# A hybrid decoder layer on one core: operands placed on whole lines, low-part products last, S5 scans joined

## The chip, the core and the metric

The kernel runs on one core of one Trainium2 chip (trn2). The metric is device time in microseconds, the median of several executions. Engines are named as in the profile: PE is TensorE's matmul, PEld its weight load, DVE is VectorE, ACT ScalarE, POOL GpSimd, SP the engine that issues most DMAs.

## The reference

One layer on `x` of 256 tokens by 2048 channels, in float32: a SwiGLU feed-forward pass, a token mixer (four mLSTM heads beside 64 groups of S5 state-space channels), a second SwiGLU pass, each added to `x`, and a last norm.

```
x = x + 0.5 * swiglu(rms_norm(x, ffn1_norm), w1, w3, w2)        # 2048 -> 5632 -> 2048
h = rms_norm(x, mix_norm);  p = h @ w_in                        # q|k, v, o, i, f, u
hm = rms_norm(mlstm_chunkwise(silu(conv(qk)), v, i, f)) * sigmoid(o)
states = associative_scan(a * s + b u)                          # S5, complex diagonal, 64 states a group
hs = glu(gelu(real(C states) + d_skip * u))
x = x + concat([hm, hs]) @ w_out
x = x + 0.5 * swiglu(rms_norm(x, ffn2_norm), ...);  out = rms_norm(x, final_norm)
```

## The kernel before

All large products are made from two parts of each operand. A weight step (`fetch`, L148 to L157) loads 1024 columns' worth of weights per partition (two K tiles of 512, in the output-gate part two of 344) into `wraw`, ScalarE rounds them into the high part `whi` (L154, type fp32r), and VectorE subtracts to get the low part `wlo` (L156). TensorE then makes three products per operand pair: high by high, high by low, low by high. Three steps are fetched ahead (`AHEAD`, L141); `wraw` has four buffers, `whi` and `wlo` three each.

`step_tok` (L159) makes a step with the token side stationary: for each of two K tiles and two token tiles it issues (xh, whi), (xh, wlo), (xl, whi), a weight tile of 512 columns as the moving operand (L174). Stationary are `xh`/`xl` (the transposed, normed input) in w1, w3 and w_in, `gh`/`gl` (the feed-forward's hidden values) in w2, and `hmh`/`hml`, `hsh`/`hsl` (the mixer's two halves) in w_out. Only the first step of the kernel has its low-part products last (`lo_last`, L169). `gemm_ch` (L210) has the weight tile stationary and 256 tokens moving (L224 to L226), for u, q and k, and for the S5 gate with `yh`/`yl` moving. `tail` (L409) finishes the last 512 output columns with moving tiles of 256 columns (L474 to L476).

The mixer (L771) runs the w_in chunks in the order u, output gate with input and forget gates, q and k, v, then w_out. Between its steps other work is hung in: `after(n, ...)` runs a function n steps later (the gates, the convolutions, the heads), and `bg` hands out the S5 work, 0.62 pieces a step. For each of eight channel groups j, S5 is: `load` (DMAs of tables), `drive` (products with the input, four multiplications on VectorE at L849 to L852 into A0, A3, A1, A2, two additions on GpSimd, L853 and L854), `scan` (eight scans of 128 elements on VectorE, L860, from A0 to A1 and from A2 to A3), `unrotate` (six operations on GpSimd, L868 to L873, through tiles B0 and B1), `emit` and `act`. The convolution of one of eight q/k tiles is four operations on VectorE (L939, L942) and a Silu. The order of instructions is left to the framework's scheduler, but for SyncE's and the start's; each engine runs its own queue in order, so a subtraction for the weights stands behind whatever VectorE was given before it.

Tiles are placed in SBUF pool by pool, in the order in which the pools are opened, each tile rounded up to 32 bytes per partition: const, xp, xTp, wrawp, whip, wlop, small, junkp, s5p, and then the pools of a phase.

Of the kernel before, what the change touches and what calls it, by code (L numbers as in the profile page):

```python
# [37 lines left out]
AHEAD = 2  # L38
WARM = 7
# [20 lines left out]
class _Layer:  # L60
# [98 lines left out]
    def step_tok(self, acc, xs, part, w, n, first, last, lo_last=False):  # L159
# [26 lines left out]
    def start(self, acc, view, gain):  # L186

        W = lambda i: self.weights(view, i * KK, KK, 0, NC)
        M = lambda i, w: self.step_tok(acc, self.xs, [(i * KK, 0), (i * KK + 1, 0)], w, NC, i == 0, i == 7, i == 0)
# [20 lines left out]
    def gemm_ch(self, acc, xs, view, nk, c0):  # L210

        nc = self.nc
        for k0 in range(0, nk, KK):
            wh, wl = self.weights(view, k0, KK, c0, NC)
            for kk in range(KK):
                k = k0 + kk
                xh, xl = xs(k)
                sp = k == nk - 1
                for nt in range(4):
                    o = acc[nt // 2][:, (nt % 2) * S:(nt % 2 + 1) * S]  # L220
                    ns = slice(nt * P, (nt + 1) * P)
                    st = k == 0 and nt % 2 == 0
                    kw = dict(skip_group_check=True)
# [9 lines left out]
    def setup(self):  # L233
# [16 lines left out]
        vec0 = self.junkp.tile([KD, P], F32, name="vec0")  # L250
# [3 lines left out]
        idle = self.junkp.tile([P, NC], F32, name="junk")  # L254
# [8 lines left out]
        self.mhalf = c.tile([P, 8], F32, name="mhalf")  # L263
# [6 lines left out]
        vecs = self.junkp.tile([rows, P], F32, name="vecs")  # L270
# [500 lines left out]
    def mixer(self, chunk_done):  # L771
# [4 lines left out]
        with ExitStack() as ctx:  # L776
            mp = self.pool("mix", ctx=ctx)
# [18 lines left out]
            uT = [mp.tile([P, 4, 2, HC], F32, name=f"uT{i}", tag=f"uT{i}") for i in range(2)]  # L796
            u4 = [mp.tile([P, 8, HC], F32, name=f"u4{i}", tag=f"u4{i}") for i in range(2)]
# [14 lines left out]
            yT = mp.tile([P, NJ, S], F32, name="yT")  # L812
            yh = mp.tile([P, NJ, S], F32R, name="yh")
            yl = mp.tile([P, NJ, S], F32R, name="yl")
# [7 lines left out]
            def s5(j):  # L822
# [3 lines left out]
                def load():  # L826
# [9 lines left out]
                    Bt = [mp.tile([P, 4, HC], F32, name=f"B{i}") for i in range(2)]  # L836
                    env["t"] = rv, w1, w2, k0, At, Bt

                def drive():
                    rv, w1, w2, k0, At, Bt = env["t"]  # L840
# [15 lines left out]
                def scan():  # L856
                    rv, w1, w2, k0, At, Bt = env["t"]
                    for a in (0, 2):
                        for q in range(4):
                            V.tensor_tensor_scan(At[a + 1][:, q, :],  # L860
                                                 self.R[:, 4 * j + q:4 * j + q + 1].broadcast_to([P, HC]),
                                                 At[a][:, q, :], 0.0, op0=ALU.mult, op1=ALU.add)

                def unrotate():
                    rv, w1, w2, k0, At, Bt = env["t"]
                    cs, sn = rv[:, 0], rv[:, 1]
                    zr, zi = At[1], At[3]
# [7 lines left out]
                def emit():  # L875
                    rv, w1, w2, k0, At, Bt = env["t"]
# [51 lines left out]
            for i, part in enumerate(self.gates(mp, gt, Dm, em)):  # L928
                self.after(1 + 4 * i, part)
# [23 lines left out]
            for hf in range(2):  # L953
                acc = self.pair()
                self.gemm_ch(acc, self.xs, win, KD, QK0 + hf * NC)
                qkp[hf] = mp.tile([P, 4, S + 3], F32, name=f"qkp{hf}", tag=f"qkp{hf}")
# [4 lines left out]
                for i in range(4):  # L961
                    self.after(1 + i, lambda hf=hf, i=i: conv(hf, i))
# [37 lines left out]
            def heads_T(c):  # L1000
                hmh[c] = mp.tile([P, 4, S], F32R, name=f"hmh{c}", tag=f"qkp{c}")
                hml[c] = mp.tile([P, 4, S], F32R, name=f"hml{c}", tag=f"vx{c}")
# [15 lines left out]
            for c in range(2):  # L1018
                v = mp.tile([P, TT, 2, DV + 1], F32, name=f"vx{c}", tag=f"vx{c}")
# [37 lines left out]
            hsh = [mp.tile([P, 4, S], F32R, name=f"hsh{i}", tag=f"uT{i}") for i in range(2)]  # L1057
            hsl = [mp.tile([P, 4, S], F32R, name=f"hsl{i}", tag=f"u4{i}") for i in range(2)]
# [26 lines left out]
    def gates(self, mp, gt, Dm, em):  # L1085
# [3 lines left out]
        rows = mp.tile([H, 4, S], F32, name="g_rows", tag="vx1")  # L1089
        more = mp.tile([H, 4, S], F32, name="g_more", tag="qkp1")  # L1090
        E = mp.tile([H, NCK, S], F32, name="g_E", tag="vx0")
# [130 lines left out]
```

## Time and profile before

| | us |
|---|---|
| median of 3 runs | 1885.29 (1884.81 to 1885.33) |
| the profiled execution | 1883.44 |
| its span, first to last instruction | 1881.7 |
| TensorE busy | 1840.2 (98%) |
| VectorE busy | 1082.8 (58%) |
| ScalarE busy | 811.5 (43%) |
| GpSimd busy | 340.3 (18%) |

The feed-forward passes fill the span up to about 760 us and from about 1145 us on; the mixer lies between. Matmul records overlap each other, since matmuls are pipelined: how fast TensorE goes is read from the distance between two starts, not from the length of a record. A mean granted clock of 1.00 is 2.4 GHz, and 0.50 is 1.2 GHz.

### The profile page before, as it was taken

Reading aid. Unit: us, or ns where it says so; the run is one execution under the profiler, and the core shown is the slowest. Engines: PE = TensorE matmul, PEld = TensorE weight load, DVE = VectorE, ACT = ScalarE, POOL = GpSimd, SP = SyncE. Lnnn points to the kernel's source line nnn. Section 1 sums busy time; section 2 is a strip of 40 time slices with the busy share of each in tenths; the row PEclk is TensorE's granted clock in tenths of the full one; section 3 lists DMA queues with packets and bytes.
Section 4 is the critical chain, followed back from the end, with each engine's and each line's share of the span. In section 5 each row is a group of like instructions: output and inputs, shape, how many; then the busy total and the mean of one; then the engine's idle time right before and its main releaser. Section 6 shows DMA issues by size and latency. Waiting matters only on the chain.

```text
span 1881.7 us, 24161 instructions
## 1 busy us (share of the span) xinstructions
PE 1840.2 (98%) x9221; PEld 1539.7 (82%) x9221; DVE 1082.8 (58%) x1335; ACT 811.5 (43%) x970; POOL 340.3 (18%) x523
## 2 busy tenths in 40 slices
PE   9999999999999999988889999999999999999998
PEld 7888888888888888987778888888888888888887
DVE  5547865555555455577888765445444444444454
ACT  6444443334444444434544455444443334444343
POOL 3000999700000000166323200000000000000011
PEclk9999999999999999999999999999999999999999
DMA  8666666666666555776766556666665566666554
GB/s 261 190 189 188 200 208 216 236 197 201 189 194 197 186 194 189 206 156 179 158 155 178 168 178 204 190 190 190 190 190 185 187 188 190 190 190 190 190 188 148
DMA packets 191252, 358.27 MB, mean 190 GB/s; under 512 B 12320, under 2 KB 29344, under 8 KB 191008
## 3 DMA queue, kind: packets, MB, share of 16 engines
q1 hardware_dynamic: 186992, 344.58, 62.2%
q0 software_dynamic: 4000, 11.10, 1.8%
q8 instruction: 72, 1.18, 0.3%
q10 hardware_dynamic: 144, 1.05, 0.1%
q14 instruction: 44, 0.36, 0.1%
HBM read 344.62 MB, written 11.01 MB: 189 GB/s over the span
## 4 chain that ended last, share of the span: by engine, by line
PE 48%; DVE 5%; issue 1%; DMA 1%; ACT 1%; POOL 0%; ACTq 0%; POOLq 0%; DVEq 0%
PE accb L174 42%; DVE wlo L156 2%; DVE A L860 1%; PE accb L226 1%; PE accb L224 1%; PE accb L225 1%; DMA wraw<-in_w_in_dram 1%; DVE qkc L942 1%; PE tpb L486 1%; PE accb L474 0%; PE accb L476 0%; PE accb L475 0%; DVE qkc L939 0%; ACT whi L154 0%; PE tpb L845 0%
## 5 line engine op out<-in xcount | busy, mean ns | idle before, releaser
L156 DVE TENSOR_TENSOR wlo<-wraw,whi 128x1024 fp32r<-128x1024 f32 (+1 forms) x630 | 788.6, 1254 | 736.6 <-ACT whi L154 736.0
L154 ACT CAST whi<-wraw 128x1024 fp32r<-128x1024 f32 (+1 forms) x630 | 655.0, 1041 | 950.9 <-PE accb L174 856.9
L174 PE MATMUL accb<-wlo,xh 128*128 128x512 f32 (+1 forms) x1568 | 606.2, 387 | 17.1 <-DVE wlo L156 17.1
L174 PE MATMUL accb<-whi,xh 128*128 128x512 f32 (+1 forms) x1568 | 609.7, 389 | 0.0
L174 PE MATMUL accb<-whi,xl 128*128 128x512 f32 (+1 forms) x1568 | 605.6, 387 | 0.0
L174 PEld LDWEIGHTS accb<-wlo,xh 128*128 128x128 f32 x1568 | 296.0, 189 | 76.4 <-DVE wlo L156 20.1
L174 PEld LDWEIGHTS accb<-whi,xl 128*128 128x128 f32 x1568 | 296.2, 189 | 57.9
L174 PEld LDWEIGHTS accb<-whi,xh 128*128 128x128 f32 x1568 | 295.9, 189 | 58.0 <-ACT whi L154 1.1
L174 PE MATMUL accb<-whi,gh 128*128 128x512 f32 x664 | 263.7, 397 | 0.0
L174 PE MATMUL accb<-whi,gl 128*128 128x512 f32 x664 | 262.4, 395 | 0.0
L174 PE MATMUL accb<-wlo,gh 128*128 128x512 f32 x664 | 262.3, 395 | 0.0
L174 PEld LDWEIGHTS accb<-whi,gl 128*128 128x128 f32 x664 | 124.7, 188 | 30.2
L174 PEld LDWEIGHTS accb<-whi,gh 128*128 128x128 f32 x664 | 124.7, 188 | 29.7
L174 PEld LDWEIGHTS accb<-wlo,gh 128*128 128x128 f32 x664 | 124.7, 188 | 29.6
L1186 POOL TENSOR_TENSOR x<-x,fn 128x512 f32<-128x512 f32 x6 | 8.9, 1500 | 699.6 <-ACT junk L317 699.6
L696 POOL TENSOR_TENSOR tr<-s5rot,sp 128x128 f32<-128x128 f32 (+6 forms) x112 | 62.1, 555 | 151.9 <-DVE sp L636 148.4
L226 PE MATMUL accb<-xh,wlo 128*128 128x256 f32 x256 | 73.6, 288 | 6.6 <-DVE wlo L156 6.6
L224 PE MATMUL accb<-xh,whi 128*128 128x256 f32 x256 | 73.9, 289 | 0.0
L225 PE MATMUL accb<-xl,whi 128*128 128x256 f32 x256 | 73.0, 285 | 0.0
L757 POOL DMA_DIRECT2D spillw<-s5w x16 | 8.6, 541 | 274.6 <-ACT s5w L728 259.7
L697 POOL TENSOR_TENSOR tr<-s5rot,sp 128x128 f32<-128x128 f32 (+6 forms) x112 | 57.8, 517 | 0.0
L226 PEld LDWEIGHTS accb<-xh,wlo 128*128 128x128 f32 x256 | 49.6, 194 | 7.6 <-DVE wlo L156 7.6
(312 smaller groups left out, 1416.3 us busy)
## 6 DMA issues: line engine op xcount, KB each, us to landing
wraw<-in_ffn_w_dram SPq DMA_DIRECT2D x528, 512.0 KB, 3.7
wraw<-in_w_in_dram SPq DMA_DIRECT2D x48, 512.0 KB, 5.3
wraw<-in_w_out_dram SPq DMA_DIRECT2D x32, 512.0 KB, 3.7
wraw<-in_w_in_dram SPq DMA_DIRECT2D x24, 344.0 KB, 5.6
spillrot<-s5rot POOLq DMA_DIRECT2D x8, 512.0 KB, 5.3
spillw<-s5w POOLq DMA_DIRECT2D x16, 256.0 KB, 4.2
s5rot<-spillrot SPq DMA_DIRECT2D x8, 512.0 KB, 7.8
wraw<-in_w_glu_dram SPq DMA_DIRECT2D x8, 512.0 KB, 3.9
```

Of the source, the lines that this page charges most:

```text
L154: nc.scalar.copy(hi, raw)
L156: nc.vector.tensor_sub(lo, raw, hi.bitcast(F32))
L174: nc.tensor.matmul(acc[t][:, :n], lhsT=x, rhs=wt, start=first and t not in seen, stop=last and t not in left)
L224: nc.tensor.matmul(o, lhsT=wh[:, kk, ns], rhs=xh, start=st, stop=False, **kw)
L225: nc.tensor.matmul(o, lhsT=wh[:, kk, ns], rhs=xl, start=False, stop=False, **kw)
L226: nc.tensor.matmul(o, lhsT=wl[:, kk, ns], rhs=xh, start=False, stop=sp, **kw)
L486: nc.tensor.transpose(b[:, o:o + P], s[t][:, kt * P:(kt + 1) * P], self.ident)
L696: G.tensor_tensor(tr[0][:, :, :k], rv[:, 0, :, 0:k], u0, op=ALU.mult)
L697: G.tensor_tensor(tr[1][:, :, :k], rv[:, 1, :, 0:k], u1, op=ALU.mult)
L860: V.tensor_tensor_scan(At[a + 1][:, q, :], self.R[:, 4 * j + q:4 * j + q + 1].broadcast_to([P, HC]), At[a][:, q, :], 0.0, op0=ALU.mult, op ...
L942: V.scalar_tensor_tensor(o, src[:, w:w + S], self.col("conv_w", w * 8 + j), o, op0=ALU.mult, op1=ALU.add)
L1186: nc.gpsimd.tensor_tensor(self.x[c][:, t, :], self.x[c][:, t, :], self.fn[:, c * NC:(c + 1) * NC], op=ALU.mult)
```

## The change

Four edits.

*Order of products.* `step_tok` puts all products with `whi` first and those with `wlo` behind them in every step; `gemm_ch` does the same. `lo_last` is gone.

*Layout.* Pads and moves of tiles change where tiles start: `mhalf` takes 256 bytes more, `junk` 448 more, `vec0` and `vecs` move from the junk pool into the buffers of `s5k0`; the mixer's large tiles (`uT`, `u4`, `yT`, `yh`, `yl`, `qkp`, `vx` and the tiles that take their places) get a pool `ma` of their own, opened before `mix`, with `qkp` and `vx` padded to 1152 elements (`WIDE`); `dg` shares the buffers of `th`.

*S5 scans.* Four scans of 128 elements become one of 512, in place, with the factors in a tile `Rt` whose first column of each 128 is zero, so that the state starts anew there. ScalarE fills `Rt` once per j. B0 and B1 are no longer tiles of their own: `unrotate` writes its intermediate products into A1 and A3.

*Convolutions.* They are hung in at every second step (`1 + 2 * i`) instead of every step.

```diff
@@ step_tok
-        todo = []
+        todo, late = [], []
         for kk, (k, _) in enumerate(part):
             xh, xl = xs(k)
             for t in range(TT):
                 ts = slice(t * P, (t + 1) * P)
-                todo += [(t, xh[:, ts], wh[:, kk, :]), (t, xh[:, ts], wl[:, kk, :]), (t, xl[:, ts], wh[:, kk, :])]
-        if lo_last:
-            todo = todo[0::3] + todo[2::3] + todo[1::3]
+                todo += [(t, xh[:, ts], wh[:, kk, :]), (t, xl[:, ts], wh[:, kk, :])]
+                late += [(t, xh[:, ts], wl[:, kk, :])]
+        todo += late
@@ gemm_ch
                 for nt in range(4):
-                    nc.tensor.matmul(o, lhsT=wh[:, kk, ns], rhs=xh, start=st, stop=False, **kw)
-                    nc.tensor.matmul(o, lhsT=wh[:, kk, ns], rhs=xl, start=False, stop=False, **kw)
-                    nc.tensor.matmul(o, lhsT=wl[:, kk, ns], rhs=xh, start=False, stop=sp, **kw)
+                    st = k0 + kk == 0 and nt % 2 == 0
+                    nc.tensor.matmul(o(nt), lhsT=wh[:, kk, ns(nt)], rhs=xh, start=st, stop=False, **kw)
+                    nc.tensor.matmul(o(nt), lhsT=wh[:, kk, ns(nt)], rhs=xl, start=False, stop=False, **kw)
+            for kk in range(KK):
+                xh, xl = xs(k0 + kk)
+                sp = k0 + kk == nk - 1
+                for nt in range(4):
+                    nc.tensor.matmul(o(nt), lhsT=wl[:, kk, ns(nt)], rhs=xh, start=False, stop=sp, **kw)
@@ setup
-        vec0 = self.junkp.tile([KD, P], F32, name="vec0")
+        vec0 = self.s5p.tile([KD, P], F32, name="vec0", tag="s5k0")
-        idle = self.junkp.tile([P, NC], F32, name="junk")
+        idle = self.junkp.tile([P, NC + 112], F32, name="junk")[:, :NC]
-        self.mhalf = c.tile([P, 8], F32, name="mhalf")
+        self.mhalf = c.tile([P, 72], F32, name="mhalf")[:, :8]
-        vecs = self.junkp.tile([rows, P], F32, name="vecs")
+        vecs = self.s5p.tile([rows, P], F32, name="vecs", tag="s5k0")
@@ mixer
+            ma = self.pool("mixa", ctx=ctx)
             mp = self.pool("mix", ctx=ctx)
-                    dg = tp2.tile([P, P], F32, name="dg")
+                    dg = tp2.tile([P, S], F32, name="dg", tag="th")[:, :P]
-            uT = [mp.tile([P, 4, 2, HC], F32, name=f"uT{i}", tag=f"uT{i}") for i in range(2)]
+            uT = [ma.tile([P, 4, 2, HC], F32, name=f"uT{i}", tag=f"uT{i}") for i in range(2)]
...
+            Rt = [mp.tile([P, 4, HC], F32, name=f"Rt{i}") for i in range(2)]
+            for i in range(2):
+                G.memset(Rt[i][:, :, 0:1], 0.0)
@@ s5: load, scan, unrotate
-                    Bt = [mp.tile([P, 4, HC], F32, name=f"B{i}") for i in range(2)]
+                    A.copy(Rt[j % 2][:, :, 1:],
+                           self.R[:, 4 * j:4 * j + 4].unsqueeze(2).broadcast_to([P, 4, HC - 1]))
                     for a in (0, 2):
-                        for q in range(4):
-                            V.tensor_tensor_scan(At[a + 1][:, q, :],
-                                                 self.R[:, 4 * j + q:4 * j + q + 1].broadcast_to([P, HC]),
-                                                 At[a][:, q, :], 0.0, op0=ALU.mult, op1=ALU.add)
+                        x = At[a].rearrange("p q c -> p (q c)")
+                        V.tensor_tensor_scan(x, Rt[j % 2].rearrange("p q c -> p (q c)"), x, 0.0,
+                                             op0=ALU.mult, op1=ALU.add)
-                    zr, zi = At[1], At[3]
+                    zr, zi, Bt = At[0], At[2], (At[1], At[3])
@@ q and k
-                qkp[hf] = mp.tile([P, 4, S + 3], F32, name=f"qkp{hf}", tag=f"qkp{hf}")
+                qkp[hf] = ma.tile([P, WIDE], F32, name=f"qkp{hf}", tag=f"qkp{hf}")[:, :4 * (S + 3)].rearrange("p (j s) -> p j s", j=4)
-                    self.after(1 + i, lambda hf=hf, i=i: conv(hf, i))
+                    self.after(1 + 2 * i, lambda hf=hf, i=i: conv(hf, i))
```

## Rows read from the trace of the kernel before

**Rows 1.** The page: busy us (share of the span) xinstructions.

```profile
PE 1840.2 (98%) x9221; PEld 1539.7 (82%) x9221; DVE 1082.8 (58%) x1335; ACT 811.5 (43%) x970; POOL 340.3 (18%) x523
```

**Rows 2.** Waits on TensorE: who <- for whom: us in total, times, longest.

```profile
PE accb L174 <- DVE wlo L156: 18.4, 11, 5.1
PE accb L226 <- DVE wlo L156: 6.6, 5, 2.9
PE tpb L1105 <- DVE gt L924: 3.3, 1, 3.3
```

**Rows 3.** Stages: length, busy PE, PEld, DVE, ACT, POOL, clock, DMA share, GB/s.

```profile
780.00:1055.00 275.00, 245.05 (x1681) 220.04 (x1680) 220.65 (x324) 111.42 (x153) 124.55 (x93) 0.98 0.68 169
820.00:862.00 42.00, 31.58 (x235) 28.65 (x234) 29.70 (x37) 11.97 (x18) 23.12 (x18) 0.95 0.76 143
900.00:960.00 60.00, 53.68 (x400) 49.23 (x399) 53.22 (x96) 26.30 (x33) 18.50 (x15) 0.97 0.68 156
```

**Rows 4.** The same view of two stretches below full clock.

```profile
857.00:866.00 9.00, 6.78 (x27) 6.78 (x28) 7.88 (x9) 2.64 (x6) 7.77 (x6) 0.62 0.46 112
939.00:944.00 5.00, 5.00 (x32) 5.00 (x31) 5.00 (x8) 1.78 (x3) 0.00 (x0) 0.66 0.84 225
```

**Rows 5.** The chain that ended last, pieces: start us, us, what.

```profile
1145.00 43.54 PE accb L174 x192
...
1454.85 90.19 PE accb L174 x387
...
1106.02 11.24 PE accb L174 x48
...
1847.28 0.11 PE accb L474
...
1860.54 0.11 PE accb L474
```

**Rows 6.** Timeline of TensorE: start us, us, instruction; first and last of 24, of 21.

```profile
787.37 0.28 PE L224 MATMUL accb<-xh,whi 128*128 128x256 f32 x1
...
790.25 0.28 PE L224 MATMUL accb<-xh,whi 128*128 128x256 f32 x1
...
1062.81 0.39 PE L174 MATMUL accb<-whi,hml 128*128 128x512 f32 x1
...
1067.67 0.40 PE L174 MATMUL accb<-whi,hml 128*128 128x512 f32 x1
```

**Rows 7.** Groups of weight loads, whole span: xcount | busy us, mean ns | idle before.

```profile
L174 PEld LDWEIGHTS accb<-whi,xl 128*128 128x128 f32 x1568 | 296.2, 189 | 57.9
```

**Rows 8.** Timeline of ACT and DVE in an undisturbed w2 step: [idle before <-releaser].

```profile
1501.32 1.05 ACT L154 CAST whi<-wraw 128x1024 fp32r<-128x1024 f32 x1 [1.75 <-PE accb L174]
1502.40 1.23 DVE L156 TENSOR_TENSOR wlo<-wraw,whi 128x1024 fp32r<-128x1024 f32 x1 [1.57 <-ACT whi L154]
```

**Rows 9.** Timeline around the longest wait on TensorE.

```profile
853.68 4.73 DVE L860 TENSOR_TENSOR_SCAN A<-R,A 128x128 f32<-128x128 f32 x8 [0.81 <-POOL A L853]
...
859.23 0.65 PE L174 MATMUL accb<-wlo,xh 128*128 128x344 f32 x1 [5.11 <-DVE wlo L156]
```

**Rows 10.** Two lines with scans: ns min/median/max, first and last start.

```profile
L860 DVE TENSOR_TENSOR_SCAN A<-R,A x64: 391/394/1518, 803.0 to 1039.8; 128x128 f32<-128x128 f32 x64
...
L1115 DVE TENSOR_TENSOR_SCAN g_rows<-g_more,g_rows x1: 678/678/678, 895.9 to 895.9; 4x256 f32<-4x256 f32 x1
```

**Rows 11.** Groups of VectorE and ScalarE in the mixer, 790 to 1056 us.

```profile
L942 DVE SCALAR_TENSOR_TENSOR qkc<-qkp,cols,qkc 128x256 f32<-128x256 f32 x24 | 18.0, 775 | 0.0
L939 DVE TENSOR_SCALAR qkc<-qkp,cols 128x256 f32<-128x256 f32 x8 | 7.0, 891 | 0.0
...
L1025 ACT ACTIVATE vx<-accb,rstd 128x512 f32<-128x512 f32 x4 | 2.6, 684 | 1.0 <-PE accb L174 1.0
```

**Rows 12.** Timeline: the last GpSimd operation of a group, the next group's second multiplication.

```profile
815.13 1.79 POOL L873 TENSOR_TENSOR S<-B,B 128x512 f32<-128x512 f32 x1
...
818.96 0.68 DVE L850 TENSOR_TENSOR A<-tpb,s5rot 128x512 f32<-128x512 f32 x1
```

More of the change, by code (lines that the diff above doesn't have):

```diff
@@ L38 @@
 AHEAD = 2
+WIDE = 1152
 WARM = 7
@@ L157, in fetch, with step_tok @@
         return hi.rearrange("p (k n) -> p k n", n=n), lo.rearrange("p (k n) -> p k n", n=n)
-    def step_tok(self, acc, xs, part, w, n, first, last, lo_last=False):
+    def step_tok(self, acc, xs, part, w, n, first, last):
         nc = self.nc
         wh, wl = w
-        todo = []
+        todo, late = [], []
         for kk, (k, _) in enumerate(part):
@@ L793, in mixer @@
             self.after(7, make_rB)
-            uT = [mp.tile([P, 4, 2, HC], F32, name=f"uT{i}", tag=f"uT{i}") for i in range(2)]
-            u4 = [mp.tile([P, 8, HC], F32, name=f"u4{i}", tag=f"u4{i}") for i in range(2)]
+            uT = [ma.tile([P, 4, 2, HC], F32, name=f"uT{i}", tag=f"uT{i}") for i in range(2)]
+            u4 = [ma.tile([P, 8, HC], F32, name=f"u4{i}", tag=f"u4{i}") for i in range(2)]
             def evac_u(hf, acc):
@@ L810, in evac_u @@
                                             in_=uT[hf][q * 32:(q + 1) * 32, :, ta, :])
-            yT = mp.tile([P, NJ, S], F32, name="yT")
-            yh = mp.tile([P, NJ, S], F32R, name="yh")
-            yl = mp.tile([P, NJ, S], F32R, name="yl")
+            yT = ma.tile([P, NJ, S], F32, name="yT")
+            yh = ma.tile([P, NJ, S], F32R, name="yh")
+            yl = ma.tile([P, NJ, S], F32R, name="yl")
             Ss = [mp.tile([P, 4, HC + 1], F32, name=f"S{i}") for i in range(2)]
@@ L927, in mixer @@
             em = mp.tile([P, TT, H], F32, name="em")
-            for i, part in enumerate(self.gates(mp, gt, Dm, em)):
+            for i, part in enumerate(self.gates(ma, mp, gt, Dm, em)):
                 self.after(1 + 4 * i, part)
@@ L1000, in heads_T @@
             def heads_T(c):
-                hmh[c] = mp.tile([P, 4, S], F32R, name=f"hmh{c}", tag=f"qkp{c}")
-                hml[c] = mp.tile([P, 4, S], F32R, name=f"hml{c}", tag=f"vx{c}")
+                hmh[c] = ma.tile([P, 4, S], F32R, name=f"hmh{c}", tag=f"qkp{c}")
+                hml[c] = ma.tile([P, 4, S], F32R, name=f"hml{c}", tag=f"vx{c}")
                 for half in range(2):
@@ L1018, in mixer @@
             for c in range(2):
-                v = mp.tile([P, TT, 2, DV + 1], F32, name=f"vx{c}", tag=f"vx{c}")
+                v = ma.tile([P, WIDE], F32, name=f"vx{c}", tag=f"vx{c}")[:, :4 * (DV + 1)].rearrange("p (t h d) -> p t h d", t=TT, h=2)
                 G.memset(v[:, :, :, DV:], 1.0)
@@ L1054, in mixer @@
             self.drain_bg()
-            hsh = [mp.tile([P, 4, S], F32R, name=f"hsh{i}", tag=f"uT{i}") for i in range(2)]
-            hsl = [mp.tile([P, 4, S], F32R, name=f"hsl{i}", tag=f"u4{i}") for i in range(2)]
+            hsh = [ma.tile([P, 4, S], F32R, name=f"hsh{i}", tag=f"uT{i}") for i in range(2)]
+            hsl = [ma.tile([P, 4, S], F32R, name=f"hsl{i}", tag=f"u4{i}") for i in range(2)]
             def evac_glu(hf, acc):
@@ L1083, in mixer, with gates @@
                 chunk_done(c)
-    def gates(self, mp, gt, Dm, em):
+    def gates(self, ma, mp, gt, Dm, em):
         nc = self.nc
         V, G, A = nc.vector, nc.gpsimd, nc.scalar
-        rows = mp.tile([H, 4, S], F32, name="g_rows", tag="vx1")
-        more = mp.tile([H, 4, S], F32, name="g_more", tag="qkp1")
-        E = mp.tile([H, NCK, S], F32, name="g_E", tag="vx0")
+        rows = ma.tile([H, 4, S], F32, name="g_rows", tag="vx1")
+        more = ma.tile([H, 4, S], F32, name="g_more", tag="qkp1")
+        E = ma.tile([H, NCK, S], F32, name="g_E", tag="vx0")
         li, f, bc, M = (rows[:, i, :] for i in range(4))
```

23 lines of the change are left out of this document (10 added, 13 removed).

## The prediction

> **What bounds the kernel now.** First the busy shares [rows 1]: TensorE is busy in 1840.2 of 1881.7 us, so time can only come from its idle 41.5 us or from a shorter distance between two matmuls. Then the waits on TensorE [rows 2]: 25.0 us are waits for the low parts `wlo` that VectorE makes (L156), 3.3 us one wait for the gates. Then the stages [rows 3]: nearly all of this lies between 780 and 1055 us, in the mixer: of these 275 us TensorE is busy in 245.05, VectorE in 220.65. Then the granted clock [rows 4]: a stretch of 9 us shows a mean of 0.62, and two of 5 us (939 to 944, 973 to 978, the first is shown) 0.66, so part of each ran at 1.2 GHz, each around one of the longer waits. The lost share is 9 x 0.38 + 2 x 5 x 0.34 = 6.8 us, at most, since TensorE also idled in them.
>
> Last, the distance of matmuls, which the busy share does not show (records overlap: 387 ns long, less than 240 apart). In unbroken pieces of the chain, none of which ever leaves TensorE [rows 5], 192 products with `xh`, `xl` of 512 columns take 43.54 us, 226.8 ns each; 387 products with `gh`, `gl` take 90.19 us, 233.0 each; 48 with `hsh`, `hsl` 11.24 us, 234.2 each; 21 with `hmh`, `hml` 4.86 us, 231.4 each [rows 6]. Shape, type, clock and moving tiles are the same in all four. What differs is where the stationary tile lies. Adding up the tile sizes of the pools, `xh`, `xl`, `whi` and `wlo` start 256 bytes past a multiple of 512, `gh`/`gl` 320, `hsh`/`hsl` 352, `hm` tiles 0, 32 and 96. A 512-column product at one column a cycle of 2.4 GHz is 213.3 ns, so each has 13.5 to 21 ns on top, and the least where the start is a multiple of 256. With 256 columns (106.7 ns) it is 24 products in 2.88 us for the channel-major steps, 120.0 ns each [rows 6], and 39 triples in 13.26 us at the end of the kernel, 113.3 each [rows 5].
>
> **The change, part by part.**
>
> *Layout.* No instruction is added. By the pad sizes (`mhalf` 256 bytes, `junk` and its neighbours 576 less, `WIDE`, the pool `ma`) the weights, `xT`, `gh` and `gl` all start at multiples of 2048 bytes afterwards, the mixer's operands at multiples of 512. I take it that every stationary tile then behaves as the best placed one does now: `gh`/`gl` products go from 233.0 to 226.8 ns: 3 x 664 (by the loops) x 6.2 = 12.4 us; `hs` 3 x 64 x 7.4 = 1.4 us; `hm` 3 x 64 x 4.6 = 0.9 us. **14.7 us.** The `xh` products, 256 past before and 0 after, I leave at 226.8: no row shows an operand pair at 0, and `hml1`, the one tile at 0 now (among neighbours at 32), runs at the 231.4 of its group. Bounds: nothing gained, and a gain or loss of one step more on all products (rivals).
>
> *High parts first.* The same 12 (or 24) products a step in another order, each with a weight load of its own before and after [rows 7]; that the loads stay hidden I take from the 189 ns a load takes beside distances of 227 and more. What moves is when things are needed and freed. A step needs `wlo` at its 9th product instead of the 2nd, 7 x 227 ns = 1.6 us later (17th instead of 3rd of 24: 14 x 120 = 1.7 us; in the 344-column steps 1.1 us). `whi` comes free 4 products, 0.9 us, earlier, so the cast starts earlier: in the steady state the cast waits 1.75 us for TensorE and the subtraction 1.57 us for the cast [rows 8], so both have that much to spare. `wlo` comes free one product, 0.2 us, later; behind the subtraction that waits for it, VectorE holds the next S5 or convolution operation, and the 1.57 us cover it.
>  Where TensorE waits only because its operand stood behind a group of other VectorE work, this shift is a gain; where VectorE has more work than time, it is gained once. The stage from 820 to 862 us is of the first kind (VectorE 29.70 of 42), 900 to 960 of the second (53.22 of 60) [rows 3]. The longest wait shows the first kind: eight scans end at 858.41, then the subtraction, and the second product of the step starts at 859.23, 5.11 us late [rows 9]; needed 1.1 us later it is still about 4 us late. Of 25.0 us of `wlo` waits I take 10 away: 6 of the output-gate steps' 10.4, 3 of the 12 in the two q/k steps and the v step behind them, 1 of the rest. The ends: 3 us if nearly all is throughput, 22 if each wait gets its shift. Of the clock's 6.8 us I take 4; ends 0 and 6.8.
>
> *Scans end to end.* 64 scans of 128 become 16 of 512. The nearest rows [rows 10]: 391 to 394 ns for one of 128 alone, 678 for one of 256, so about (678 - 394)/128 = 2.2 ns an element, and for 512 an estimate of 678 + 256 x 2.2 = 1.25 us. In the trace eight take 4.73 us [rows 9], of which the first and the fifth lose about 1.1 us each beside GpSimd (1.5 for 0.39). Two of 1.25 us that lose the same are 4.7: **hardly less**. Ends: 2 us less of VectorE per channel group if one such loss goes, 1 us more if a longer scan meets a second GpSimd operation. I take 1 us on TensorE. Added: eight copies of R on ScalarE over 508 elements, nearest row 684 ns for 512 [rows 11], hidden in ScalarE's idle time (busy 111.42 of 275 us there [rows 3]); ahead of a cast one would delay it by less than the 1.75 us it has to spare. The two small GpSimd memsets are worth 0.2 us on an engine that idles there.
>
> *B tiles taken over by A1 and A3.* The next group's second VectorE multiplication now waits for the last GpSimd operation of the group before (L873) instead of the one ahead of it. In the closest case L873 ends at 816.92 and L850 starts at 818.96 [rows 12]: 2.0 us of cover. Without it up to the 1.79 us of L873 a group, with the weight subtractions queued behind on VectorE.
>
> *Convolutions every second step.* The same 32 VectorE operations; four groups spread over eight steps instead of four. Each is about 0.89 + 3 x 0.775 = 3.2 us beside GpSimd [rows 11]. The last one is now due one step before the scores that read it; VectorE runs a step or two ahead of TensorE, so I cost it at nothing; if it does not, TensorE waits up to 3 us once, with the next chunk's products behind it. The spread takes peaks off, which is part of the 3 us above. The gates' wait of 3.3 us comes from the same crowding: I take 1 us off.
>
> **Sum**: 14.7 + 10 + 4 + 1 + 1 = 30.7 us. The profiled execution took 1883.4 us (span 1881.7), the median of the runs is 1885.3, 1.9 above; 1885.3 - 30.7 gives **1854 us**, with its own range of 1840 to 1866.
>
> **The rivals.**
>
> *Whole lines help every product.* If a read that starts at a multiple of 512 saves the same step again, all large products gain: (3 x 1472 + 3 x 664 + 3 x 128) x 6.7 + 960 x 6.7 = 52 us on top, **1802 us**. For it: the excess goes in steps of about 6.7 ns (113.3 against 106.7, 120.0 and 226.7 with twice, 233.3 with three times that). Against it: `hml1`. The Trainium skill's page "TensorE: Matmul & The Clock Gate" (section on 56 and 53.3 ns) puts the distance at columns over 2.4 GHz plus about 2.5 ns; by that floor the sum would be some 84 us lower than mine, 1770 us, an estimate, and no fp32r row here comes that near.
>
> *The layout moves nothing.* The differences come from something other than the start, say the distance of the two tiles. For it: at the kernel's end the same `gh` tiles at 320 run at 113.3 ns, the least excess of all. Then 16 us are left of the sum: **1869 us**. A page speaks for this: the Trainium skill's "SBUF — State Buffer" (section Specifications) has lines of 16 bytes; all these tiles already start on them, so by it the pads change nothing. The 226.8 and 233.0 ns of equal shapes say that some coarser unit matters.
>
> *Slower: all operands start alike and meet.* Stationary and moving tiles now both start at 0, and if two reads then fall on the same place, products with `xh` take what those with `gh` take now: 3 x 1472 x 6.2 = 27 us more, and `gh`, `hm`, `hs` gain nothing. With the 16 us gained in the mixer that is **1896 us**. It decides from a distance of about 230.4 ns for `xh` (16 us over 4416 products). For it: `hml1` at 0 is no faster; against it: today's `xh` products have equal offsets in both tiles and are the fastest of their shape.
>
> *No net effect*: mixer waits refill, because VectorE's 220.65 of 275 us are unchanged, and the layout moves nothing: 1882 to 1889.
>
> **Chances.** Forecast 0.46, every product faster 0.28, layout idle 0.14, slower 0.08, no net effect 0.04. The low end, 1775, stops short of the floor; the high end, 1874, takes in the third case. About 0.2%, 3.8 us, is what a measurement can tell from no change: faster 0.88, same 0.04, slower 0.08.
>
> **What would show it.** In the profile after: products with `gh` 226 to 227 ns apart (right), 233 (the layout is idle), near 220 with `xh` too (second rival), `xh` above 230 (slower). Waits for `wlo` near 15 us instead of 25, at most one or two stretches below full clock. L860 16 times at 1.3 to 2.4 us. I would be most wrong in the size of the step per product: 1 ns on all large products is 7 us.

## The result, and the profile after

The changed kernel takes **1861.9 us** (1860.8 to 1862.4, 4 runs) against 1885.3 for the kernel before in the same comparison: ratio 0.9874, 95% interval 0.9862 to 0.9886. The forecast was 1854, with a range of its own of 1840 to 1866; 22.6 us of the span went (1881.7 to 1859.1) instead of 30.7. The kernels further down were timed in other comparisons, in which the kernel before took 1883.0 to 1885.3 us, so a difference of one of them from 1861.9 is good to about 2 us. Line numbers of the changed kernel are one to nine higher: the cast is L155, the subtraction for the low parts L157, the product L175, the scan L869, the gates' transposes L1113.

The page's busy time of TensorE (share of the span, instructions) and the windows view of the mixer, same columns as [rows 3]:

```profile
PE 1826.6 (98%) x9221; PEld 1541.4 (83%) x9221; DVE 1072.0 (58%) x1287; ACT 817.7 (44%) x977; POOL 346.6 (19%) x525
...
780.00:1055.00 275.00, 254.17 (x1742) 227.71 (x1741) 218.44 (x283) 118.28 (x164) 125.23 (x93) 0.96 0.69 174
```

The same instructions of TensorE (9221) take 13.6 us less busy time, and 9.0 us of its idle time are gone (41.5 to 32.5). VectorE issues 48 instructions fewer (the joined scans) at nearly the same busy time, and in the mixer's window it is as busy as it was (218.44 of 275 us, 220.65 before). The mean clock in that window fell, 0.98 to 0.96.

Pieces of the chain that ended last, to be set beside [rows 5] (start us, us, what), and of TensorE's timeline the first and the 31st product of the kernel's end:

```profile
1100.84 10.90 PE accb L175 x48
...
1127.11 43.54 PE accb L175 x192
...
1393.59 174.10 PE accb L175 x768
```

```profile
1822.23 0.28 PE L477 MATMUL accb<-whi,gh 128*128 128x256 f32 x1
...
1825.82 0.28 PE L477 MATMUL accb<-whi,gh 128*128 128x256 f32 x1
```

48 products with `hs` are 227.1 ns apart (234.2 before), 192 with `xh`, `xl` 226.8 as before, and a piece of 768, most of them with `gh`, `gl`, 226.7 (233.0 before). That is the layout term as forecast. But the 256-column products at the end, 30 of them in 3.59 us, are now 119.7 ns apart and were 113.3: here the kernel lost something.

The waits on TensorE (who <- for whom: us in total, times, longest), beside [rows 2]:

```profile
PE accb L175 <- DVE wlo L157: 6.8, 7, 2.0
PE accb L175 <- ACT whi L155: 5.9, 4, 2.3
PE tpb L1113 <- DVE gt L932: 5.5, 2, 4.5
...
PE tpb L1154 <- DVE Dm L1159: 2.1, 1, 2.1
```

25.0 us of waits for low parts became 6.8, where 15 had been forecast, but waits for the *high* parts (5.9) and for the gates' matrix `Dm` (2.1) are new, and the gates' sums went from 3.3 to 5.5: of the 18.2 us that went, 10.2 stand again in other rows.

By stage, from the first product of one to the first of the next, read from the starts in the two traces:

| stage | before, us | after, us | difference |
|---|---|---|---|
| four w2 stages of the feed-forward passes | 475.5 | 462.6 | -12.9 |
| w_out with hs | 47.6 | 46.2 | -1.3 |
| w_out with hm (1.4 us of it idle time) | 54.5 | 51.9 | -2.6 |
| the kernel's end | 35.3 | 36.8 | +1.6 |
| u | 51.5 | 49.9 | -1.6 |
| output gate | 68.9 | 66.0 | -2.9 |
| q, k | 67.7 | 66.2 | -1.5 |
| v | 65.1 | 63.5 | -1.6 |
| S5 gate, all w1 and w3 stages | 1007.7 | 1007.6 | -0.1 |

The first four rows, without the 1.4 us of idle, are the layout's: 13.9 us. The idle and the stages from u to v are the rest: 9.1 us, where 16 had been forecast.

### The profile page after: what moved, and what is told of

Read it like the earlier page. It is cut to its first block, busy times and chain, and to the rows that moved or that the text cites. A ratio compares the mean times of both kernels' runs of the same rounds, so it can differ in the third digit from the quotient of the medians.

```text
span 1859.1 us, 24158 instructions
## 1 busy us (share of the span) xinstructions
PE 1826.6 (98%) x9221; PEld 1541.4 (83%) x9221; DVE 1072.0 (58%) x1287; ACT 817.7 (44%) x977; POOL 346.6 (19%) x525
## 4 chain that ended last, share of the span: by engine, by line
PE 93%; DVE 3%; DMA 1%; issue 1%; ACT 0%; POOL 0%; SPq 0%; ACTq 0%; DVEq 0%; POOLq 0%
PE accb L175 83%; PE accb L223 2%; PE accb L224 2%; PE accb L229 2%; DVE wlo L157 1%; PE tpb L489 1%; DMA wraw<-in_w_in_dram 1%; DVE A L869 1%; PE tpb L338 1%; PE tpb L854 0%; PE accb L479 0%; PE accb L478 0%; PE accb L477 0%; DMA u<-uT 0%; PE tpb L893 0%
## 5 line engine op out<-in xcount | busy, mean ns | idle before, releaser
L157 DVE TENSOR_TENSOR wlo<-wraw,whi 128x1024 fp32r<-128x1024 f32 (+1 forms) x630 | 789.9, 1256 | 691.5 <-ACT whi L155 689.3
L155 ACT CAST whi<-wraw 128x1024 fp32r<-128x1024 f32 (+1 forms) x630 | 656.5, 1043 | 926.3 <-PE accb L175 817.5
L175 PE MATMUL accb<-whi,xh 128*128 128x512 f32 (+1 forms) x1568 | 610.1, 389 | 5.9 <-ACT whi L155 5.9
L175 PE MATMUL accb<-whi,xl 128*128 128x512 f32 (+1 forms) x1568 | 605.6, 386 | 0.0
L175 PE MATMUL accb<-wlo,xh 128*128 128x512 f32 (+1 forms) x1568 | 414.7, 386 | 6.8 <-DVE wlo L157 6.8
L175 PEld LDWEIGHTS accb<-whi,xh 128*128 128x128 f32 x1568 | 295.6, 189 | 64.8 <-ACT whi L155 7.2
L175 PEld LDWEIGHTS accb<-wlo,xh 128*128 128x128 f32 x1568 | 293.2, 189 | 66.7 <-DVE wlo L157 8.9
L175 PEld LDWEIGHTS accb<-whi,xl 128*128 128x128 f32 x1568 | 296.0, 189 | 56.5
L175 PE MATMUL accb<-whi,gh 128*128 128x512 f32 x664 | 259.8, 391 | 0.0
L175 PE MATMUL accb<-whi,gl 128*128 128x512 f32 x664 | 258.4, 389 | 0.0
L175 PE MATMUL accb<-wlo,gh 128*128 128x512 f32 x664 | 177.5, 389 | 0.0
L175 PEld LDWEIGHTS accb<-wlo,gh 128*128 128x128 f32 x664 | 124.7, 188 | 25.9
L175 PEld LDWEIGHTS accb<-whi,gh 128*128 128x128 f32 x664 | 124.7, 188 | 25.5
L175 PEld LDWEIGHTS accb<-whi,gl 128*128 128x128 f32 x664 | 124.7, 188 | 25.4
L1194 POOL TENSOR_TENSOR x<-x,fn 128x512 f32<-128x512 f32 x6 | 11.9, 1999 | 689.1 <-ACT junk L320 689.1
L699 POOL TENSOR_TENSOR tr<-s5rot,sp 128x128 f32<-128x128 f32 (+6 forms) x112 | 60.4, 540 | 152.4 <-DVE sp L639 148.9
L223 PE MATMUL accb<-xh,whi 128*128 128x256 f32 x256 | 64.0, 288 | 0.0
L701 POOL TENSOR_TENSOR s5rot<-tr,tr 128x128 f32<-128x128 f32 (+6 forms) x112 | 63.0, 574 | 3.3
L224 PE MATMUL accb<-xl,whi 128*128 128x256 f32 x256 | 63.5, 285 | 0.0
L700 POOL TENSOR_TENSOR tr<-s5rot,sp 128x128 f32<-128x128 f32 (+6 forms) x112 | 52.2, 467 | 0.0
L223 PEld LDWEIGHTS accb<-xh,whi 128*128 128x128 f32 x256 | 49.4, 193 | 1.0 <-issue 0.9
```

The lines of the kernel that those rows point to most:

```text
L155: nc.scalar.copy(hi, raw)
L157: nc.vector.tensor_sub(lo, raw, hi.bitcast(F32))
L175: nc.tensor.matmul(acc[t][:, :n], lhsT=x, rhs=wt, start=first and t not in seen, stop=last and t not in left)
L223: nc.tensor.matmul(o(nt), lhsT=wh[:, kk, ns(nt)], rhs=xh, start=st, stop=False, **kw)
L224: nc.tensor.matmul(o(nt), lhsT=wh[:, kk, ns(nt)], rhs=xl, start=False, stop=False, **kw)
L699: G.tensor_tensor(tr[0][:, :, :k], rv[:, 0, :, 0:k], u0, op=ALU.mult)
```

## Experiments

**Each half alone.** First the order of products put into the kernel before, then the layout alone.

```diff
# e1_order: kernel before, with step_tok (shown) and gemm_ch of the changed one
+                todo += [(t, xh[:, ts], wh[:, kk, :]), (t, xl[:, ts], wh[:, kk, :])]
+                late += [(t, xh[:, ts], wl[:, kk, :])]
+        todo += late
...
# e2_layout: kernel before, with only the pads, the pool ma and the moved tiles
+        self.mhalf = c.tile([P, 72], F32, name="mhalf")[:, :8]
+        idle = self.junkp.tile([P, NC + 112], F32, name="junk")[:, :NC]
+            ma = self.pool("mixa", ctx=ctx)
...
```

> The kernel before with one part of the change alone: products with the high parts first, those with the low parts last; layout, scans and convolutions as before. Theory (the order is what shortens the mixer's waits; the layout acts only on the distance of products): products with gh stay near 233 ns apart, the mixer loses 7 to 9 us, 1876 to 1879 us. Rival (the mixer's gain of the whole change comes from the thinned-out VectorE work, the spread convolutions and joined scans): the order alone moves under 2 us, 1883 us or more.

> The kernel before with the layout alone: tiles start where they start in the changed kernel; order of products, scans and convolutions as before. Theory: every 512-column product at 226.8 ns, the 240 products at the kernel's end at 120.0 ns instead of 113.3, the waits of the mixer as before: 12.9 us less in w2, 2.2 less in w_out, 1.6 more at the end, 1871 to 1873 us. Rival (the layout also lengthens or shortens the waits, because TensorE gets through its products faster while VectorE doesn't): over 3 us away from that.

The order alone: 1879.5 us against 1884.5, ratio 0.9978 (0.9967 to 0.9988), 5.0 us, just short of the 1876 to 1879 of its theory. The layout alone: 1870.6, just under the 1871 to 1873 of its theory, ratio 0.9928 (0.9913 to 0.9942), 13.9 us, with an interval of 11 to 16; the table has 13.9. Waits on TensorE of the order alone, then the first of the layout alone:

```profile
PE accb L174 <- DVE wlo L156: 13.5, 7, 4.9
PE tpb L1107 <- DVE gt L926: 5.6, 1, 5.6
PE accb L228 <- DVE wlo L156: 2.3, 1, 2.3
PE accb L174 <- ACT whi L154: 2.1, 2, 1.5
PE tpb L1148 <- DVE Dm L1153: 1.5, 1, 1.5
```

```profile
PE accb L175 <- DVE wlo L157: 18.4, 11, 5.1
```

With the layout alone this row is that of [rows 2], so the layout leaves the waits for low parts as they were. With the order alone the two rows for `wlo` fall from 25.0 to 15.8, nearly the 15 that the prediction named, but the gates' wait grows by 2.3, 2.1 for the high parts and 1.5 for `Dm` are new, and the stage q, k is 0.7 us *longer* than before. So the order does what it says, and 5.9 of the 9.2 us come back in other waits.

**Each of the two small edits taken out of the changed kernel.**

```diff
# e4_noconv
-                    self.after(1 + 2 * i, lambda hf=hf, i=i: conv(hf, i))
+                    self.after(1 + i, lambda hf=hf, i=i: conv(hf, i))
# e5_noscan
-                        V.tensor_tensor_scan(x, Rt[j % 2].rearrange("p q c -> p (q c)"), x, 0.0,
+                        for q in range(4):
+                            V.tensor_tensor_scan(At[a + 1][:, q, :], ...
```

> The changed kernel with one part undone: the convolutions at every step again instead of every second. Theory: the spread is worth 1 to 3 us in the q/k and v steps, 1863 to 1865 us. Rival (VectorE has as much to do either way, so spreading gains nothing, and it put the scores' inputs later): within 1 us of the changed kernel or faster, 1860 to 1862 us.

> The changed kernel with one part undone: eight scans of 128 elements again instead of two of 512, B tiles of their own, no copies of R. Theory: 1 us of gain at most from the joined scans, 1861 to 1864 us. Rival (fewer operations to wait beside GpSimd free 2 us of VectorE per channel group): 4 us slower than the changed kernel or more, 1866 us.

Without the spread of the convolutions 1863.1 us (0.9889, 0.9872 to 0.9905), without the joined scans 1862.5 (0.9884, 0.9870 to 0.9899). Both intervals overlap that of the whole change: 1.3 and 0.7 us by the medians, neither of them told from nothing; the scans' forecast of 1 us is not contradicted, nor is it shown. In the first, the v stage of the profiled execution takes 66.6 us instead of 63.5 and no other stage moves by more than 0.7. Order and layout alone add up to 18.9 us, with these two to 20.9, of 23.4; the 2.5 us left over lie within the intervals of the parts.

**What in the layout counts.** The pads made every tile start at a multiple of 512, and they made stationary and moving tile of each product start *alike*. To tell these apart, one kernel shifts everything by 64 bytes together, and two others give the stationary tiles starts of their own, the weights staying at 0. Each of the three was run once.

```diff
# o3_all64: one pad ahead of all pools, all tiles at 64 past a multiple of 512
-        self.mhalf = c.tile([P, 72], F32, name="mhalf")[:, :8]
+        self.mhalf = c.tile([P, 88], F32, name="mhalf")[:, :8]
# o1_offsets: xh0..xh3 (and xl) at 0, 64, 128, 192 bytes; the gh/gl pairs at steps of 64 from 256
+        t = self.xTp.tile([P, 4 * S + pad], F32R, name=f"{nm}{c}")
+                    g2 = gp.tile([P, 8 * S + GSTEP], F32R, name="g2")
...
# o2_offsets: the same with xh0..xh3 at 32, 96, 160, 224, the gh/gl pairs at steps of 32 from 80
```

> The changed kernel with every matmul operand moved by 64 bytes: weights, xh, xl, gh, gl and the mixer's operands all start 64 bytes past a multiple of 512, none on a whole line. Theory (the relative start of stationary and moving tile counts): all 512-column products stay at 226.8 ns, 256-column ones at 120.0, time as the changed kernel's, 1862 us. Rival (a stationary row has to lie on whole lines of 256 or 512 bytes): 233 ns for all 512-column products, 6792 x 6.4 ns = 43 us slower, 1905 us.

> The changed kernel with other starts of the stationary tiles: xh and xl of chunk c (c = 0 to 3) start c x 64 bytes past a multiple of 512, gh and gl of buffer b (0 to 5) at 256 + b x 64, the mixer's operands at 256; weights stay at 0. So one run shows the distance of 512-column products for eight relative starts, of 256-column products with the weight stationary for 0, -64, -128, -192, and at the kernel's end for gh at 256 to 512. Theory A (a coarse line of 256 bytes counts: a stationary row of 512 bytes touches two such lines or three): 0 and 256 give 226.8 ns, all others 233. Theory B (what counts is the start of one operand relative to the other): a graded set of distances, with some starts below 226.8 ns, since the end of the kernel ran at 113.3 ns for 256 columns with +64 and 120.0 with 0.

> As the run with offsets in steps of 64 bytes, with the starts between: xh and xl of chunk c at 32, 96, 160, 224 bytes past a multiple of 512, gh and gl of buffer b at 80, 112, 144, 176, 208, 240, the mixer's operands at 64, weights at 0. If the distance goes with the relative start modulo 256 as the first run shows (0: 226.8 ns, 64: 233 to 234, 128: 232, 192: 229), 32 to 160 should give 230 to 234 and 208 to 240 values between 226 and 229; a start with less than 226 ns would be a better layout than the changed kernel's. If only whole 64-byte steps count, 32 should behave as 0 and 96 as 64.

All 64 past a multiple of 512: 1861.4 us, as the changed kernel, and in the chain the same distances (226.9 and 226.7 ns):

```profile
1260.56 43.57 PE accb L175 x192
...
1393.90 174.13 PE accb L175 x768
```

Different starts: 1882.2 us with steps of 64 bytes (all but 0.7 us of the time before) and 1900.8 with starts of 32 and more. One w1 or w3 chunk of the first of them, in TensorE's timeline, the first product with each of `xh0` to `xh3`, and the next chunk's first; 24 products lie between two rows:

```profile
1153.96 0.39 PE L177 MATMUL accb<-whi,xh 128*128 128x512 f32 x1
...
1159.41 0.40 PE L177 MATMUL accb<-whi,xh 128*128 128x512 f32 x1
...
1165.01 0.39 PE L177 MATMUL accb<-whi,xh 128*128 128x512 f32 x1
...
1170.58 0.39 PE L177 MATMUL accb<-whi,xh 128*128 128x512 f32 x1
...
1176.09 0.39 PE L177 MATMUL accb<-whi,xh 128*128 128x512 f32 x1
```

227.1 ns apart at 0, 233.3 at 64, 232.1 at 128, 229.6 at 192 bytes between the starts of the stationary and the moving tile. Over the whole trace, products whose neighbours have the same difference (distances above 300 ns left out): 227.2, 233.4, 232.3 and 229.3 with `xh`. The trace does not name the buffers of `gh`. In the order of their use the six pairs show 227.6, 233.4, 227.8, 229.0, 232.7 and 233.3; this agrees with `xh` if the pool hands them out as 256, 576, 512, 448, 384, 320, and they are read so here: 0 and 256 alike, 64 and 320 alike. The kernel before fits in too: 233.0 at 64 (`gh`), 234.2 at 96 (`hs`).

In the other kernel `xh` has 233.1 at 32, 234.1 at 96, 233.6 at 160 and 233.4 at 224; the `gh` pairs, read in the same order, 227.8 at 240, 16 short of the next 256, 231.9 at 208 and 230.2 at 176. So the distances are no smooth curve, and the guess that all starts from 208 to 240 lie below 229 was wrong. For products of 512 columns the **difference of the two starts, modulo 256 bytes,** is what counts. No start and no difference in any kernel here gave a mean below 226.7; the theory that some would is wrong as well.

This is shown for runs of products that share one difference. The order alone has a mixed run: its layout is that of the kernel before, and the last 24 products with `hm` use `hmh1` (at 32) and `hml1` (at 0, so 0 from the weights modulo 256), mostly in turns. Two of them, 12 products apart:

```profile
1058.27 0.40 PE L174 MATMUL accb<-whi,hml 128*128 128x512 f32 x1
...
1061.08 0.40 PE L174 MATMUL accb<-whi,hml 128*128 128x512 f32 x1
```

That is 234.2 ns, no less than 32 alone has (233.1): here the well placed tile gains nothing among its neighbours. Why, the runs don't tell.

For 256 columns the order is another one: 120 at differences of 0, 116 to 120 at most others, and 113 to 114.5 at single ones (+64 with `gh` at the end of the kernel before, 320 with weights stationary and 448 with `gh` in the kernel with steps of 64, where +64 gave 117.8). What decides there, the runs don't tell.

**What holds up the mixer: VectorE's work, or GpSimd beside it?** In the changed kernel the v stage stands still twice, around 960 us. The timeline of VectorE, then GpSimd, ahead of it:

```profile
950.52 2.32 DVE L157 TENSOR_TENSOR wlo<-wraw,whi 128x1024 fp32r<-128x1024 f32 x1
952.76 1.51 DVE L950 SCALAR_TENSOR_TENSOR qkc<-qkp,cols,qkc 128x256 f32<-128x256 f32 x1
954.20 1.38 DVE L947 TENSOR_SCALAR qkc<-qkp,cols 128x256 f32<-128x256 f32 x1
955.50 2.93 DVE L950 SCALAR_TENSOR_TENSOR qkc<-qkp,cols,qkc 128x256 f32<-128x256 f32 x2
958.35 1.21 DVE L157 TENSOR_TENSOR wlo<-wraw,whi 128x1024 fp32r<-128x1024 f32 x1
...
959.88 0.47 DVE L950 SCALAR_TENSOR_TENSOR qkc<-qkp,cols,qkc 128x256 f32<-128x256 f32 x1
```

```profile
950.30 1.46 POOL L877 TENSOR_TENSOR A<-A,s5rot 128x512 f32<-128x512 f32 x1 [1.16 <-DVE A L869]
951.84 2.16 POOL L878 TENSOR_TENSOR S<-A,A 128x512 f32<-128x512 f32 x1
954.07 1.35 POOL L879 TENSOR_TENSOR A<-A,s5rot 128x512 f32<-128x512 f32 x1
955.39 1.34 POOL L880 TENSOR_TENSOR A<-A,s5rot 128x512 f32<-128x512 f32 x1
956.81 1.34 POOL L881 TENSOR_TENSOR S<-A,A 128x512 f32<-128x512 f32 x1
```

A convolution tap takes 1.4 to 1.5 us while GpSimd runs and 0.47 right behind it; the two engines go in turns, one operation each. The subtraction at 958.35, for which TensorE waits at 959.6, stands behind four taps. Three kernels test it, all from the changed one: three of the four taps left out (24 operations of VectorE missing); the first tap of each convolution moved to ScalarE (nothing missing); four of the six operations of the second rotation left out on GpSimd (VectorE's and TensorE's instructions as they were).

```diff
# e6_onetap: taps 0 to 2 of each convolution are missing
-                for w in range(3):
+                for w in range(0):
# f2_tapact
-                V.tensor_scalar(o, src[:, 3:3 + S], self.col("conv_w", 24 + j), self.col("conv_b", j), ...
+                A.activation(o, src[:, 3:3 + S], AF.Identity, scale=self.col("conv_w", 24 + j), bias=...
# f4_unrot2: the six operations become these two; the difference and the sum are missing
-                    ...
+                    G.tensor_tensor(Ss[0][:, :, 1:], zr, cs, op=ALU.mult)
+                    G.tensor_tensor(Ss[1][:, :, 1:], zi, sn, op=ALU.mult)
```

> The changed kernel without three of the convolution's four taps (24 VectorE operations, 18.0 us in the kernel before, are left out). Theory (in the q/k and v steps VectorE has more work than time, so waits taken away there come back at the next thing that needs it): the idle time of TensorE in these 32 steps falls from 11.9 us to under 5. Rival (single operations stand in the way, whatever the load): it stays above 9 us.

> The changed kernel with the first of the four taps of each convolution computed by ScalarE (scale and bias of an activation) instead of VectorE: 8 operations of about 0.8 to 0.9 us leave VectorE, 8 of about 0.4 us come to ScalarE. Leaving out 24 operations of VectorE gave 7 us, of which 4.3 were idle time of TensorE in the v stage and 2.8 the lower clock behind it. Theory (VectorE's work is the limit there): 8/24 of that, 2 to 3 us less than 1861.9. Rival (the taps matter only where one stands ahead of a weight's low part, and ScalarE's casts are now delayed instead): within 1 us of 1861.9, with more waits for the high parts.

> The changed kernel with four of GpSimd's six operations of each channel group's second rotation left out (two products are written straight to the states; the other two products, the difference and the sum are missing). VectorE and TensorE issue what they issued before. While this chain of GpSimd runs (950 to 958 us of the changed kernel), VectorE's convolution taps take 1.4 to 1.5 us each, 0.38 us right behind it, and the low part that TensorE waits for at 960 us stands behind them. Theory (VectorE is slow only while GpSimd works, and that makes the wait): the four us of idle in the v stage and the lower clock behind it go, the output-gate and q/k stages lose 2 to 4 us of idle as well; 1850 to 1855 us. Rival (the number of VectorE's operations counts, not how long one takes beside GpSimd): the v stage within 1 us of 63.5, the time above 1859.

Without the taps 1854.7 us in its one run, 7 less than the changed kernel (6 if each is set against the kernel before in its own comparison), and all of it in the v stage: 63.5 to 56.4 us. The idle time of TensorE in the q/k and v steps fell from 11.9 to 6.8 us, between the theory's 5 and the rival's 9: the v stage lost all of its own, q and k nearly kept theirs (7.6 and 6.8). With a tap on ScalarE 1861.2 (0.9879, 0.9864 to 0.9894): nothing, where a third of the 7 had been expected; the rival's time, though not its reason, since the waits for high parts are 5.7 us where they were 5.9. With GpSimd's chain cut to two operations 1852.7 (0.9831, 0.9815 to 0.9848), 9.1 less by the medians and 8 by the ratios: the v stage 57.2 us, the output gate 2.2 less, q and k 1.2 more. The v stage in the windows view, of the changed kernel, of that without taps and of that with the short chain:

```profile
936.00:999.50 63.50, 59.17 (x331) 48.83 (x330) 53.24 (x71) 26.62 (x41) 25.75 (x16) 0.95 0.60 145
```

```profile
936.90:993.20 56.30, 56.30 (x330) 47.35 (x329) 46.90 (x59) 23.61 (x39) 27.22 (x16) 1.00 0.67 160
```

```profile
934.40:991.60 57.20, 56.74 (x331) 47.34 (x330) 47.99 (x72) 28.17 (x43) 13.57 (x9) 1.00 0.67 163
```

In both, TensorE stands for under half a microsecond instead of 4.3, and the clock stays at full speed: the 4.3 us of idle cost 2 to 3 us more through the lower clock after them. VectorE's *number* of operations is the same in the last and its busy time 5 us less. So the number does not decide alone: what counts is how long the operations ahead of the subtraction take, and beside GpSimd they take longer. (A shorter chain also hands its tiles on earlier; no run keeps the two apart.) Why a tap moved to ScalarE gave nothing, the timeline of that kernel shows:

```profile
951.50 2.32 DVE L157 TENSOR_TENSOR wlo<-wraw,whi 128x1024 fp32r<-128x1024 f32 x1
953.74 5.80 DVE L950 SCALAR_TENSOR_TENSOR qkc<-qkp,cols,qkc 128x256 f32<-128x256 f32 x4
959.46 1.21 DVE L157 TENSOR_TENSOR wlo<-wraw,whi 128x1024 fp32r<-128x1024 f32 x1
```

Between the same two subtractions there are four taps again: the scheduler put the next convolution's into the place that came free, beside GpSimd, at 1.45 us each.

What the last run does not bear out: the idle time of the output-gate and q/k stages was to fall by 2 to 4 us, and went from 16.0 to 15.7. Of the 2.2 us of the output gate 0.7 are idle time; the rest came with its clock (a mean of 1.00 where it was 0.97). The waits there have other causes, of which the chain of the changed kernel may show one, 10.5 us of a load of weights, and the cast behind it:

```profile
829.76 10.52 DMA wraw<-in_w_in_dram
840.38 0.77 ACT whi L155
```

**The gates.** Their wait can be moved: the three parts two weight steps later each.

```diff
# f1_gates (f3_both: this and the tap on ScalarE)
-                self.after(1 + 4 * i, part)
+                self.after(3 + 4 * i, part)
```

> The changed kernel with the three parts of the gates due two weight steps later each (after steps 3, 7 and 11 instead of 1, 5 and 9); nothing else differs, and every engine does the same work. The changed kernel shows 5.5 us of waits for the gates' sums (longest 4.5) and 2.1 us for Dm in the q/k stage, and 10.2 us at the lower clock there. Theory (VectorE's work in the q/k and v stages sets the time, and a wait that is moved comes back in another place): the gates' wait falls below 1 us, but others grow; the idle time of TensorE from the output gates to the end of v stays within 3 us of the 20.3 us it is, and the time falls by less than 2.5 us from 1861.9. Rival (the order in which the parts are due sets the waits): 5 us or more of idle go, the stretch at the lower clock gets shorter by 3.4 us or more, and the time falls by 6 to 8 us.

> Both of the edits of f1 and f2 in the changed kernel. If VectorE's work is the limit, the sum is little more than the taps' share: 1857 to 1860 us. If the order of the parts is, 1852 to 1856.

With the gates moved 1867.4 us (0.9911, 0.9894 to 0.9927), **5.6 slower** than the changed kernel by the medians, 7 by the ratios; with the tap as well 1869.5 (0.9921, 0.9906 to 0.9936). Waits on TensorE in the q/k stage of the first:

```profile
PE tpb L1154 <- DVE Dm L1159: 6.1, 1, 6.1
PE tpb L1144 <- DVE g_mp L1130: 3.7, 1, 3.7
PE tpb L1144 <- DVE g_more L1137: 1.3, 1, 1.3
PE tpb L1144 <- DVE g_E L1133: 1.0, 3, 0.4
```

The waits for `gt` and `Dm` had been 7.6 us; now it is 12.1: the second part now asks for sums that VectorE has not made, and `Dm` comes behind the convolutions of the first q/k half while GpSimd rotates. Both theories had missed that it could get *worse*: the idle time of q, k and v was 11.9 us and is 16.9. The place that the parts had was better than it looked.

## Why the prediction came out as it did

- **Layout, 14.7 us: right in size, for a reason that does not hold.** `gh`/`gl` and `hs` went to 226.7 to 227.1 ns as named, `hm` to 227.4, `xh` stayed; 15.4 us. Left out of the sum was the end of the kernel, at 113.3 ns in [rows 5]: the prediction used it as an argument for a rival and did not ask what becomes of it. It cost 1.6, so the net is 13.9.
- **The reason given, "the least where the start is a multiple of 256", was the wrong one that fits.** The kernel shifted by 64 bytes has no such start and loses nothing. It is the difference of the two starts; `xh` against the weights had 0 already (256 and 256), `gh` 64, `hs` 96. That the size came out all the same was luck: the pads gave every tile a whole line and every pair the difference 0 in one, so both rules say the same of this change.
- **`hml1`** was taken as an argument against a gain at 0. The 21 products of [rows 6] are of `hmh1` (32) and `hml1` (0) alone, 14 and 7; at 233.1 and 226.8 ns each, an estimate from the products of one difference, the mean would be 231.0, and it is 231.4. So [rows 6] does not speak against the rule; but the mixed run above, at 234.2, shows that such a mean need not come out.
- **Whole lines help every product (1802): wrong**, `xh` stayed where it was. **Operands that start alike meet (1896): wrong**, alike is best for 512 columns. For 256 columns it is among the worst seen (120 ns), so a part of that rival was there, in 240 products instead of 4416. **Layout moves nothing (1869): wrong.** It drew on the 16-byte lines in the Trainium skill's page "SBUF — State Buffer" (section Specifications); by these traces the lines are not all that counts: all starts lie on them, and equal products differ by 7 ns. The floor of the Trainium skill's page "TensorE: Matmul & The Clock Gate" (section "Wait — 56ns, not 53.3ns?"), 215.8 ns for 512 columns as an estimate from its rule, was reached by no product of this type: 226.7 is the least mean in the traces of before, after and the three kernels with shifted starts.
- **Waits for low parts, 10 us: the step that was mis-sized is the split into two kinds.** They fell by 18.2, the longest (5.11 in [rows 9]) to 2.0. But the prediction counted waits of one row and took them as gains. The first kind of wait (an operand behind a group) does go, and then the *next* thing behind the same group is late: the cast, the gates' sums, `Dm`. Net it is 9.1 us, of which the order alone gave 5.0. What had been summed as 12 (10 for these waits, 1 each for the gates and the scans) came out as 9.1, with the gates 4.3 worse.
- **Clock, 4 us: nothing came of it.** The mean clock in the mixer's window went from 0.98 to 0.96, in the q/k stage from 0.97 to 0.92 (windows view of the changed kernel):

```profile
869.80:936.00 66.20, 58.61 (x490) 55.02 (x490) 54.44 (x97) 34.33 (x44) 30.05 (x23) 0.92 0.70 171
```

  The prediction tied the low clock to the *longest* waits ([rows 4]). These got shorter, but the records of the granted clock show 1.2 GHz at four places now, each around a wait of TensorE (from 841.6, 875.8, 913.3 and 961.1 us on), 20.5 us together, where they show 13.7 us in the mixer before. Shorter waits are not what brought that: with the layout alone, whose waits for low parts are those of before, the records show 20.5 us too, with the order alone 17.1. From u to w_out with hm, without the layout's share, time and idle time fell by the same 9.1 us, so nothing was gained from the clock. This is what separates 30.7 from the 22.6 of the span: 4 here, 2.9 in waits, 1.6 at the end, less 0.7 that the layout gave more; 0.4 is a later start.
- **Scans: right in what they take.** The 1 us on TensorE is within the noise of the run without them. Joined, a scan takes (ns, minimum, median, maximum; first and last start; shape):

```profile
L869 DVE TENSOR_TENSOR_SCAN A<-Rt,A x16: 1193/2284/2311, 794.9 to 1022.7; 128x512 f32<-128x512 f32 x16
```

1.19 us alone (1.25 estimated) and 2.28 beside GpSimd (2.4 named as the upper end). It loses 1.1 us once each as the short ones did, so two of them are hardly less than eight.
- **Costed at nothing, and rightly:** the copies of R (0.62 us), the reuse of A1 and A3 (VectorE never sat idle ahead of its second multiplication, L859), the later convolutions (no wait for scores shows).

## What to carry to other kernels

When equal matmuls run at different distances, compare the *pair* of addresses, the stationary tile's and the moving tile's, before a rule on one of them; and list every product that uses a tile before moving it, since what is best for 512 columns was among the worst for 256. A wait that is named by an operand goes on record under that operand's name only; when it is removed, count what else stands behind the same group of work, and take as gain the change of all waits of the stage. An operation taken off a crowded engine frees a slot and not time, if the scheduler fills the slot with another one and the slow partner (here GpSimd) runs on beside it.

## What the hardware showed that was not expected

- **TensorE, fp32r.** 512 columns, in runs of one difference: 226.7 to 227.8 ns where the two tiles' starts differ by 0 modulo 256 bytes, 233 to 234 at 64, 232 to 233 at 128, 229 at 192. How mixed runs go stays open. 256 columns: 113 to 120, with another order that stays open.
- **VectorE beside GpSimd.** A tap of 256 elements 0.47 us alone, 1.45 beside GpSimd's 512-element operations; a `TENSOR_SCALAR` with one tile as input 0.40 and 1.38. Taking four of the six operations of GpSimd's chain away was worth 8 to 9 us of the kernel's time, though GpSimd is busy for 19% of the span. That a VectorE operation with two SBUF inputs waits for a GpSimd operation that reads SBUF to end, and the other way round, is in the Trainium skill's page "SBUF — State Buffer" (section "Who interferes with whom"); the turns in the two timelines agree.
- **A part of the program hung in later** made the kernel 5.6 us slower by the medians, with the same work on every engine.
